# Turning h and the residual in the wide phases: TensorE transposes against 32 x 32 squares on VectorE

## The chip, the cores and the metric

The kernel runs on one core of a Trainium2 chip. The metric is the device time of one execution in microseconds (us), as the median of several runs. Beside the timed runs there is one execution under the hardware profiler; its rows and its trace are what this text reads.

The engines are named as the profile names them: PE is TensorE's matmul (PEld its weight loads), DVE is VectorE, ACT is ScalarE, POOL is GpSimd, SP is SyncE, which issues most of the transfers.

## The reference: what is computed

A two-layer decoder trunk on 256 positions of width 2048, in float32. Layer 0 is a sparse attention mixer and a SwiGLU block, layer 1 a pooling mixer and a SwiGLU block; every block is preceded by an RMSNorm and added to the residual. The part that the change touches, cut to what matters (D_FF is 5632):

```python
def rms_norm(x, g):
    x32 = x.astype(jnp.float32)
    y = x32 * lax.rsqrt(jnp.mean(x32 * x32, axis=-1, keepdims=True) + EPS)
    return (y * g.astype(jnp.float32)).astype(x.dtype)
...
def swiglu(h, w_gu, w_down):
    gu = h @ w_gu
    gate, up = gu[..., :D_FF], gu[..., D_FF:]
    return (jax.nn.silu(gate) * up) @ w_down
...
        h = rms_norm(x, norm_ffn[i])
        x = x + swiglu(h, ffn_w_gu[i], ffn_w_down[i])
    return rms_norm(x, norm_final)
```

## The kernel before

All weights stream through once. SyncE loads blocks of 128 x 1024 float32 (512 KB) into five buffers `wraw`. Each block is split into two float32r numbers: ScalarE copies the high part into `whi` (L158), VectorE subtracts it and leaves the rest in `wlo` (L159). There are three pairs of `whi` and `wlo`. A product of float32 accuracy is then three matmuls: high by high, high by low, low by high.

The first 376 us or so are the attention. Behind it come the wide phases, which the change is about: output projection, SwiGLU of layer 0, pooling mixer, SwiGLU of layer 1. They are products of all 256 positions (two halves `t` of 128) with 512 columns of a weight at a time, `wide_gemm` (L207). The activations are stationary (128 x 128), a block of weights holds two steps k of 128 rows by 512 columns, and each step and half takes the three matmuls of L216, L217 and L218. A block is thus 12 matmuls. The results of the two halves stand in two banks of PSUM with the positions on the partitions.

Work moves ahead of use in `next_block` (L173): when block b is about to be used, `ahead(b)` emits the split of block b + 2 and the load of block b + 4. The split of block b + 2 can start once block b - 1 has been used, since it takes that block's pair of buffers.

A result with positions on the partitions has to be turned before it can be stationary in the next product, which contracts over its columns. This is done in two places:

- `ffn` (L752): for each of 11 groups f of 512 columns there is a gate product `pg`, a Silu on ScalarE (L760), an up product `pu`, and `h` on VectorE (L764). Then eight 128 x 128 transposes on TensorE (L771) turn the two halves of `h` into PSUM tiles `turn`, and `split_pair` (L747) makes the split `hid` of them, in two steps of 128 x 512 on ScalarE (L749) and on VectorE (L750). `hid` is what the down product contracts over, 44 steps k.
- `residual` (L719): the product is added to the residual `xs` (L724), its squares are summed (L727), and eight transposes (L737) turn the new columns into `turn`. `spread` (L250) multiplies by the gain and splits into `xg[c]`, four steps k of the next phase's operand (L253 on ScalarE, L254 on VectorE).

There are 11 groups f in each of two layers, so 22 turns of `h`, 176 transposes. The residual is turned after four products of the output projection, four of layer 0's down product and four of the pooling's output, so 12 turns, 96 transposes. The last layer's down product turns nothing. Its last 512 columns use weights that were parked ahead in `xg` (L150), and `finish` (L789) applies the last norm. `row_scale` (L706) works out 1/rms of each row during the first product of each phase that follows a norm; its result is used only behind that product.

A scheduler sets the order of instructions on each engine from the program's order and dependences. It puts the transposes of a group between the matmuls of the next product.

The last layer's final gain is loaded into the buffers of `h` while its down product runs (L778).

Of the kernel before, what the change touches and what calls it, by code (L numbers as in the profile page):

```python
# [11 lines left out]
F32 = mybir.dt.float32  # L12
F32R = mybir.dt.float32r
AF = mybir.ActivationFunctionType
OP = mybir.AluOpType
AX = mybir.AxisListType

P = 128
D = 2048
S = 256  # L20
# [11 lines left out]
FT = DFF // P  # L32
# [13 lines left out]
N5 = 512  # L46
NJ = D // N5
FJ = DFF // N5
# [19 lines left out]
def nsa_pool_trunk(ctx, tc, first, xn, small, band, gfin, w_qk, w_vg, w1k, w1v, w_o,  # L68
                   p_in, p_grp, p_out, gu, down, out):
    nc = tc.nc  # L70
# [64 lines left out]
    state = {"dma": 0, "split": 0, "used": 0, "acc": 0, "more": None, "turn": 4}  # L135
# [11 lines left out]
    def emit_split(b):  # L147
        _, n, off = stream[b]
        t = raws.pop(b)
        if b in parked:  # L150
            for c in range(2):
                hi, lo = xg[4 * parked[b] + 2 * c:4 * parked[b] + 2 * c + 2]
                w = t[:, c * N5:(c + 1) * N5]
                nc.scalar.activation(hi, w, AF.Copy)
                nc.vector.tensor_tensor(lo, w, hi.bitcast(F32), op=OP.subtract)
            return
        hi, lo = split_tiles(off)
        nc.scalar.activation(hi[:, :n], t[:, :n], AF.Copy)  # L158
        nc.vector.tensor_tensor(lo[:, :n], t[:, :n], hi[:, :n].bitcast(F32), op=OP.subtract)  # L159
        parts[b] = (hi, lo)  # L160

    def ahead(b):
# [7 lines left out]
            emit_dma(state["dma"])  # L170
            state["dma"] += 1

    def next_block():  # L173
        while True:
            b = state["used"]
            ahead(b)
            state["used"] += 1
            if b not in parked:
                return parts.pop(b)


# [22 lines left out]
                k += 1  # L204
        return ps

    def wide_gemm(rhs, own=False, apart=0):  # L207

        ps = [bank(own) for _ in range(2)]
        n = len(rhs)

        def step(k, hi, lo, t):
            xa, xb = (rhs[k][:, a * S + t * P:a * S + (t + 1) * P] for a in range(2))
            nc.tensor.matmul(ps[t], xa, hi, start=k == 0, stop=False)  # L216
            nc.tensor.matmul(ps[t], xa, lo, start=False, stop=False)  # L217
            nc.tensor.matmul(ps[t], xb, hi, start=False, stop=k == n - 1)  # L218

        for k in range(n - apart):  # L220
            if k % 2 == 0:
                w = next_block()
            for t in range(2):
                step(k, *(a[:, k % 2 * N5:(k % 2 + 1) * N5] for a in w), t)
        for t in range(2):
            for i in range(apart):
                step(n - apart + i, *xg[2 * i:2 * i + 2], t)
        return ps
# [9 lines left out]
    ident = cst.tile([P, P], F32, name="ident")  # L238
# [7 lines left out]
    xg = [xgp.tile([P, 2 * S], F32R, name=f"xg{c}") for c in range(KC)]  # L246
# [3 lines left out]
    def spread(c, x, gain):  # L250

        f = col(gain, c) if isinstance(gain, str) else gain
        nc.scalar.activation(xg[c][:, :S], x, AF.Copy, scale=f)  # L253
        nc.vector.scalar_tensor_tensor(xg[c][:, S:], x, f, xg[c][:, :S].bitcast(F32),  # L254
                                       op0=OP.mult, op1=OP.subtract)
# [447 lines left out]
    def turn():  # L703
        return psT.tile([P, 2 * S], F32, name="turn")

    def row_scale():  # L706
# [9 lines left out]
        nc.vector.tensor_tensor(t, t, a, op=OP.mult)  # L716
        nc.vector.scalar_tensor_tensor(rcol, t, 1.5, rcol, op0=OP.add, op1=OP.mult)

    def residual(j, ps, gain, gf=None):  # L719


        xc = [xs[:, t, j * N5:(j + 1) * N5] for t in range(2)]
        for t in range(2):
            nc.vector.tensor_tensor(xc[t], ps[t], xc[t], op=OP.add)  # L724
        for t in range(2):
            sq = xp.tile([P, N5], F32, name="sq", bufs=2)
            nc.scalar.activation(sq, xc[t], AF.Square, accum_out=ssq[:, t, j:j + 1])  # L727
        if gf is not None:
            for t in range(2):
                nc.gpsimd.tensor_tensor(xc[t], xc[t], gf[j], op=OP.mult)  # L730
            return
        for q in range(2):
            tr = turn()
            for i in range(2):
                for t in range(2):
                    o = (2 * q + i) * P
                    nc.tensor.transpose(tr[:, i * S + t * P:i * S + (t + 1) * P], xc[t][:, o:o + P],  # L737
                                        ident)
            for i in range(2):
                spread(4 * j + 2 * q + i, tr[:, i * S:(i + 1) * S], gain)  # L740

    def pairs(pool, n, name):

        both = [pool.tile([P, 2, 2 * S], F32R, name=f"{name}{i}") for i in range(n // 2)]
        return both, [both[c // 2][:, c % 2] for c in range(n)]

    def split_pair(dst, tr):  # L747
        src = tr.rearrange("p (c t) -> p c t", c=2)
        nc.scalar.activation(dst[:, :, :S], src, AF.Copy)  # L749
        nc.vector.tensor_tensor(dst[:, :, S:], src, dst[:, :, :S].bitcast(F32), op=OP.subtract)  # L750

    def ffn(gain, fpool):  # L752
        hid2, hid = pairs(fpool, FT, "hid")
        for f in range(FJ):
            pg = wide_gemm(xg)
            if f == 0:
                row_scale()
            sg = [fpool.tile([P, N5], F32, name=f"sg{t}", bufs=1) for t in range(2)]
            for t in range(2):
                nc.scalar.activation(sg[t], pg[t], AF.Silu, scale=rcol[:, t:t + 1])  # L760
            pu = wide_gemm(xg)
            h = [fpool.tile([P, N5], F32, name="h", bufs=4) for t in range(2)]
            for t in range(2):
                nc.vector.scalar_tensor_tensor(h[t], pu[t], rcol[:, t:t + 1], sg[t], op0=OP.mult,  # L764
                                               op1=OP.mult)
            for q in range(2):
                tr = turn()
                for i in range(2):
                    for t in range(2):
                        o = (2 * q + i) * P  # L770
                        nc.tensor.transpose(tr[:, i * S + t * P:i * S + (t + 1) * P],  # L771
                                            h[t][:, o:o + P], ident)
                split_pair(hid2[2 * f + q], tr)
        gf = None
        if gain is None:
            gf = [fpool.tile([P, N5], F32, name="h", bufs=4) for _ in range(NJ)]
            for j in range(NJ):
                nc.sync.dma_start(gf[j], gfin[:, j * N5:(j + 1) * N5])  # L778

            nc.scalar.activation(fpool.tile([P, 1], F32, name="root"), sg[1][:, 0:1], AF.Sqrt,  # L780
                                 scale=0.0, bias=eps)
        for j in range(NJ - (gf is not None)):
            residual(j, wide_gemm(hid), gain, gf)
        if gf is not None:
            ps = wide_gemm(hid, apart=2 * PARK)
            for t in range(2):
                finish(t, ps[t], gf[NJ - 1], fpool)
# [26 lines left out]
                out[t * P:(t + 1) * P, i * N5:(i + 1) * N5], y)  # L814

    for j in range(NJ):
        residual(j, wide_gemm(oT, own=j == 0), "g_ffn0")
    op.close()

    with tc.tile_pool(name="f0", bufs=1, reuse_waits="tile") as fpool:  # L820
# [3 lines left out]
    with tc.tile_pool(name="pl", bufs=1, reuse_waits="tile") as pl:  # L824
# [8 lines left out]
        mixed = [pl.tile([P, 2 * S], F32R, name=f"mixed{c}") for c in range(KC)]  # L833

        def pool_group(g, first):
            ps = wide_gemm(xg)
            if first:
                row_scale()
            uh = [pl.tile([P, N5], F32R, name=f"uh{t}", bufs=2) for t in range(2)]
            ul = [pl.tile([P, N5], F32R, name=f"ul{t}", bufs=2) for t in range(2)]  # L840
            for t in range(2):
                r = rcol[:, t:t + 1]
                nc.scalar.activation(uh[t], ps[t], AF.Copy, scale=r)
                nc.vector.scalar_tensor_tensor(ul[t], ps[t], r, uh[t].bitcast(F32), op0=OP.mult,
                                               op1=OP.subtract)
            for q in range(2):
                tr = turn()
                for i in range(2):
                    a = slice((2 * q + i) * P, (2 * q + i + 1) * P)
                    d = tr[:, i * S:(i + 1) * S]  # L850
                    nc.tensor.matmul(d, uh[0][:, a], bh[:, g, :S], start=True, stop=False)
                    nc.tensor.matmul(d, ul[0][:, a], bh[:, g, :S], start=False, stop=False)
                    nc.tensor.matmul(d[:, :CS], uh[0][:, a], bl[:, g], start=False, stop=False)
                    nc.tensor.matmul(d[:, P:], uh[1][:, a], bh[:, g, S:], start=False, stop=False)
                    nc.tensor.matmul(d[:, P:], ul[1][:, a], bh[:, g, S:], start=False, stop=True)
                split_pair(pooled2[2 * g + q], tr)
# [19 lines left out]
        mix_group(GROUPS[-1])  # L876
        rhs = [mixed[4 * g + c] for g in GROUPS for c in range(4)]
        for j in range(NJ):
            residual(j, wide_gemm(rhs), "g_ffn1")

    with tc.tile_pool(name="f1", bufs=1, reuse_waits="tile") as fpool:
        ffn(None, fpool)
# [124 lines left out]
```

## Time and profile before

| | |
|---|---|
| median of 3 runs | 2127.1 us (2126.83 to 2128.48) |
| the profiled execution | 2126.66 us |
| its span, first to last instruction | 2124.9 us |
| granted TensorE clock | 0.999 |
| TensorE matmul busy | 2110.7 us, 99% |
| VectorE busy | 1182.8 us, 56% |
| ScalarE busy | 1030.0 us, 48% |
| transfers | 396.93 MB, 187 GB/s |

Matmuls are pipelined: a row's length is its latency and overlaps the next one's, so the time that an instruction takes from the stream is read from start to start. Each row of a group of instructions gives: line, engine, operation, output and inputs, shapes, count, then busy us, mean ns of one, and the idle time of the engine ahead of them with what ended it. A row of a timeline gives start and length in us.

### The profile page before, as it was taken

Reading aid. Unit: us, or ns where it says so; the run is one execution under the profiler, and the core shown is the slowest. Engines: PE = TensorE matmul, PEld = TensorE weight load, DVE = VectorE, ACT = ScalarE, POOL = GpSimd, SP = SyncE. Lnnn points to the kernel's source line nnn. Section 1 sums busy time; section 2 is a strip of 40 time slices with the busy share of each in tenths; the row PEclk is TensorE's granted clock in tenths of the full one; section 3 lists DMA queues with packets and bytes.
Section 4 is the critical chain, followed back from the end, with each engine's and each line's share of the span. In section 5 each row is a group of like instructions: output and inputs, shape, how many; then the busy total and the mean of one; then the engine's idle time right before and its main releaser. Section 6 shows DMA issues by size and latency. Waiting matters only on the chain.

```text
span 2124.9 us, 28354 instructions
## 1 busy us (share of the span) xinstructions
PE 2110.7 (99%) x10922; PEld 1810.6 (85%) x10922; DVE 1182.8 (56%) x1555; ACT 1030.0 (48%) x1492; POOL 53.6 (3%) x103
## 2 busy tenths in 40 slices
PE   9999999999999999999999999999999999999998
PEld 8999999888888888888888888888888888888886
DVE  8678887554554445545445555555444554455443
ACT  6567777454444444444444455444444444444442
POOL 1001111000000000000000000000000000000000
PEclk9999999999999999999999999999999999999999
DMA  6664444666666666666666656666666666677663
GB/s 246 209 219 137 144 143 128 210 187 191 192 185 192 188 189 189 187 191 191 193 189 191 198 175 183 184 192 183 193 188 190 190 187 191 188 220 224 195 192 106
DMA packets 114537, 396.93 MB, mean 187 GB/s; under 512 B 13378, under 2 KB 17730, under 8 KB 114146
## 3 DMA queue, kind: packets, MB, share of 16 engines
q1 hardware_dynamic: 113922, 394.41, 61.6%
q8 instruction: 85, 1.39, 0.3%
q10 hardware_dynamic: 480, 0.72, 0.1%
q14 instruction: 50, 0.41, 0.1%
HBM read 391.25 MB, written 2.16 MB: 185 GB/s over the span
## 4 chain that ended last, share of the span: by engine, by line
PE 98%; ACT 1%; DVE 1%; DMA 0%; issue 0%; SPq 0%; DVEq 0%
PE acc L216 27%; PE acc L218 27%; PE acc L217 27%; PE acc L194 3%; PE acc L192 3%; PE acc L193 3%; PE turn L771 1%; PE ps_o L665 1%; PE ps_t L627 1%; PE ps_s L559 1%; PE ps_s L560 1%; PE ps_s L561 1%; PE turn L737 0%; PE acc L499 0%; PE acc L500 0%; PE acc L501 0%
## 5 line engine op out<-in xcount | busy, mean ns | idle before, releaser
L159 DVE TENSOR_TENSOR wlo<-wraw,whi 128x1024 fp32r<-128x1024 f32 (+1 forms) x714 | 874.1, 1225 | 828.5 <-ACT whi L158 823.9
L158 ACT ACTIVATE whi<-wraw 128x1024 fp32r<-128x1024 f32 (+1 forms) x714 | 754.3, 1057 | 914.8 <-PE acc L218 826.8
L218 PE MATMUL acc<-whi,xg 128*128 128x512 f32 x1536 | 599.9, 391 | 0.0
L217 PE MATMUL acc<-wlo,xg 128*128 128x512 f32 x1536 | 598.8, 390 | 0.0
L216 PE MATMUL acc<-whi,xg 128*128 128x512 f32 x1536 | 546.3, 391 | 0.0
L217 PEld LDWEIGHTS acc<-wlo,xg 128*128 128x128 f32 x1536 | 288.5, 188 | 59.1
L218 PEld LDWEIGHTS acc<-whi,xg 128*128 128x128 f32 x1536 | 288.6, 188 | 58.7
L216 PEld LDWEIGHTS acc<-whi,xg 128*128 128x128 f32 x1536 | 288.6, 188 | 58.1
L217 PE MATMUL acc<-wlo,hid 128*128 128x512 f32 x688 | 268.3, 390 | 0.0
L218 PE MATMUL acc<-whi,hid 128*128 128x512 f32 x688 | 268.0, 390 | 0.0
L216 PE MATMUL acc<-whi,hid 128*128 128x512 f32 x688 | 242.0, 390 | 0.0
L192 PE MATMUL acc<-xg,whi 128*128 128x256 f32 x560 | 158.2, 286 | 0.5 <-ACT whi L327 0.3
L193 PE MATMUL acc<-xg,whi 128*128 128x256 f32 x560 | 157.2, 284 | 0.0
L194 PE MATMUL acc<-xg,wlo 128*128 128x256 f32 x560 | 154.3, 285 | 1.4 <-DVE wlo L159 1.2
L217 PEld LDWEIGHTS acc<-wlo,hid 128*128 128x128 f32 x688 | 129.2, 188 | 26.7
L218 PEld LDWEIGHTS acc<-whi,hid 128*128 128x128 f32 x688 | 129.2, 188 | 26.6
L216 PEld LDWEIGHTS acc<-whi,hid 128*128 128x128 f32 x688 | 129.2, 188 | 26.4
L192 PEld LDWEIGHTS acc<-xg,whi 128*128 128x128 f32 x560 | 105.8, 189 | 1.9 <-ACT whi L327 1.4
L193 PEld LDWEIGHTS acc<-xg,whi 128*128 128x128 f32 x560 | 105.9, 190 | 0.0
L194 PEld LDWEIGHTS acc<-xg,wlo 128*128 128x128 f32 x560 | 103.6, 189 | 2.6 <-DVE wlo L159 1.4
L587 ACT ACTIVATE prob<-prob,mx 128x128 f32<-128x128 f32 (+1 forms) x128 | 56.5, 444 | 9.9 <-DVE mx L581 6.8
L217 PE MATMUL acc<-wlo,oT 128*128 128x512 f32 x128 | 50.2, 392 | 0.0
(235 smaller groups left out, 1784.0 us busy)
## 6 DMA issues: line engine op xcount, KB each, us to landing
wraw<-in_gu SPq DMA_DIRECT2D x352, 512.0 KB, 3.7
wraw<-in_down SPq DMA_DIRECT2D x176, 512.0 KB, 3.8
wraw<-in_w_qk SPq DMA_DIRECT2D x64, 512.0 KB, 4.2
wraw<-in_w_o SPq DMA_DIRECT2D x32, 512.0 KB, 3.6
wraw<-in_p_in SPq DMA_DIRECT2D x32, 512.0 KB, 3.6
wraw<-in_p_out SPq DMA_DIRECT2D x32, 512.0 KB, 3.6
bias<-skew SPq DMA_DIRECT2D x32, 200.0 KB, 3.2
wx<-in_first SPq DMA_DIRECT2D x15, 320.0 KB, 6.6
```

The source lines that it names most:

```text
L158: nc.scalar.activation(hi[:, :n], t[:, :n], AF.Copy)
L159: nc.vector.tensor_tensor(lo[:, :n], t[:, :n], hi[:, :n].bitcast(F32), op=OP.subtract)
L192: nc.tensor.matmul(ps, hi, x[:, :S], start=first, stop=False)
L193: nc.tensor.matmul(ps, hi, x[:, S:], start=False, stop=False)
L194: nc.tensor.matmul(ps, lo, x[:, :S], start=False, stop=last)
L216: nc.tensor.matmul(ps[t], xa, hi, start=k == 0, stop=False)
L217: nc.tensor.matmul(ps[t], xa, lo, start=False, stop=False)
L218: nc.tensor.matmul(ps[t], xb, hi, start=False, stop=k == n - 1)
L559: nc.tensor.matmul(o, q[0], k[0], start=True, stop=False)
L560: nc.tensor.matmul(o, q[0], k[1], start=False, stop=False)
L561: nc.tensor.matmul(o, q[1], k[0], start=False, stop=True)
L587: nc.scalar.activation(p[:, o:o + n], p[:, o:o + n], AF.Exp, bias=mx[:, i:i + 1], accum_out=su[:, i:i + 1])
```

## The change

The turns leave TensorE. A new function `turned_squares` cuts the turn of 512 columns by 256 positions into squares of 32 x 32. One VectorE instruction (`nc.vector.transpose`, L742 in the new kernel, STREAM_TRANSPOSE in the order) reads 32 partitions of the source, eight squares wide (2 x 4 x 32 elements), transposes each square and writes it to another quarter of the partitions of one tile `flip`. 16 such instructions, for each of four source quarters and four destination quarters, make a turn. They are not emitted at once but put on a list `later`. `next_block(beside)` takes that many entries off the list behind each block's split, not ahead of the latest `wlo` instruction (`tc.issue_after`), and `wide_gemm` empties the rest of the list at its end.

- `h`: two entries a block (`beside=2`) during the next product, four during the first gate product of a phase. The split of the turned `h` is one entry at the list's end, now one step of 128 x 1024 on each of ScalarE and VectorE (`split_four`).
- the residual: 16 squares and four spreads, 20 entries, at four a block in the output projection, in the pooling phase and in the first gate products, at two a block in layer 0's down product.
- `ffn(None)`, the last layer: the list is emptied by a call of `some()` ahead of the last down product, since the buffers of `h` are then loaded with the final gain; that load is now two transfers of 512 KB instead of four of 256 KB.

```diff
+    later = []
+
+    def some(n=None):
+        with tc.issue_after(state["lo"]):
+            for f in later[:n]:
+                f()
+        del later[:n]
+
-    def next_block():
+    def next_block(beside=0):
         while True:
             b = state["used"]
             ahead(b)
             state["used"] += 1
             if b not in parked:
+                some(beside)
                 return parts.pop(b)
...
             if k % 2 == 0:
-                w = next_block()
+                w = next_block(beside)
             for t in range(2):
                 step(k, *(a[:, k % 2 * N5:(k % 2 + 1) * N5] for a in w), t)
+        some()
...
+    flip = xp.tile([P, 4, S], F32, name="flip")
+
+    def turned_squares(src, dst=flip):
+        to = dst.rearrange("p c (t i s) -> i p t c s", t=2, i=4)
+        of = src.rearrange("p t (c j s) -> j p t c s", c=4, j=4)
+        for i in range(4):
+            for j in range(4):
+                a, b = (slice(32 * q, 32 * q + 32) for q in (i, j))
+                later.append(lambda o=to[i][b], x=of[j][a]: nc.vector.transpose(o, x))
...
-        for q in range(2):
-            tr = turn()
-            for i in range(2):
-                for t in range(2):
-                    o = (2 * q + i) * P
-                    nc.tensor.transpose(tr[:, i * S + t * P:i * S + (t + 1) * P], xc[t][:, o:o + P],
-                                        ident)
-            for i in range(2):
-                spread(4 * j + 2 * q + i, tr[:, i * S:(i + 1) * S], gain)
+        turned_squares(xs[:, :, j * N5:(j + 1) * N5])
+        for c in range(4 * j, 4 * j + 4):
+            later.append(lambda c=c: spread(c, flip[:, c % 4], gain))
...
         for f in range(FJ):
-            pg = wide_gemm(xg)
+            pg = wide_gemm(xg, beside=2 if f else 4)
...
-            for q in range(2):
-                tr = turn()
-                for i in range(2):
-                    for t in range(2):
-                        o = (2 * q + i) * P
-                        nc.tensor.transpose(tr[:, i * S + t * P:i * S + (t + 1) * P],
-                                            h[t][:, o:o + P], ident)
-                split_pair(hid2[2 * f + q], tr)
+            turned_squares(h)
+            later.append(lambda f=f: split_four(hid4[f]))
         gf = None
         if gain is None:
-            gf = [fpool.tile([P, N5], F32, name="h", bufs=4) for _ in range(NJ)]
-            for j in range(NJ):
-                nc.sync.dma_start(gf[j], gfin[:, j * N5:(j + 1) * N5])
+            some()
+            gf = []
+            for j in range(0, NJ, 2):
+                g2 = fpool.tile([P, 2, N5], F32, name="h", bufs=2)
+                nc.sync.dma_start(g2, gfin[:, j * N5:(j + 2) * N5])
+                gf += [g2[:, 0], g2[:, 1]]
...
-            residual(j, wide_gemm(hid), gain, gf)
+            residual(j, wide_gemm(hid, beside=2), gain, gf)
...
-        residual(j, wide_gemm(oT, own=j == 0), "g_ffn0")
+        residual(j, wide_gemm(oT, own=j == 0, beside=4), "g_ffn0")
...
-            ps = wide_gemm(xg)
+            ps = wide_gemm(xg, beside=4)
...
-            residual(j, wide_gemm(rhs), "g_ffn1")
+            residual(j, wide_gemm(rhs, beside=4), "g_ffn1")
```

How this moves the instructions is seen in their order (line, operation, output and inputs, shape, and a count where equal ones stand in a row). TensorE, behind the first `h` of layer 0, before; `turn` is the PSUM tile, `ident` the identity:

```order
L216 MATMUL acc<-whi,xg_83 128x512
L217 MATMUL acc<-wlo,xg_83 128x512
L218 MATMUL acc<-whi,xg_83 128x512
L771 MATMUL turn<-ident,h 128x128 x2
L216 MATMUL acc<-whi,xg_83 128x512
L217 MATMUL acc<-wlo,xg_83 128x512
L771 MATMUL turn<-ident,h 128x128 x6
L218 MATMUL acc<-whi,xg_83 128x512
```

In the new kernel no row with `ident` and `h` or `xs` is left on TensorE; the matmuls stand as they stood, some with the halves t in another order. VectorE at the start of layer 0's SwiGLU, where the last turned columns of the residual become `xg_92` to `xg_95` (steps k = 12 to 15 of the product that has just begun). Before:

```order
L724 TENSOR_TENSOR xs<-acc,xs 128x512 x2
L159 TENSOR_TENSOR wlo<-wraw,whi 128x1024
L711 TENSOR_REDUCE tot<-ssq 128x2
L713 TENSOR_SCALAR na<-tot 128x2
L714 RECIPROCAL rcol<-nt 128x2
L715 SCALAR_TENSOR_TENSOR nt<-rcol 128x2
L716 TENSOR_TENSOR nt<-nt,na 128x2
L717 SCALAR_TENSOR_TENSOR rcol<-nt,rcol 128x2
L159 TENSOR_TENSOR wlo<-wraw,whi 128x1024
L254 SCALAR_TENSOR_TENSOR xg_92<-turn,sm,xg_92 128x256
L254 SCALAR_TENSOR_TENSOR xg_94<-turn,sm,xg_94 128x256
```

And in the new kernel at the same place, from the second of its five splits on:

```order
L159 TENSOR_TENSOR wlo<-wraw,whi 128x1024
L742 STREAM_TRANSPOSE flip<-xs 32x2x4x32 x4
L726 TENSOR_SCALAR na<-tot 128x2
L727 RECIPROCAL rcol<-nt 128x2
L159 TENSOR_TENSOR wlo<-wraw,whi 128x1024
L742 STREAM_TRANSPOSE flip<-xs 32x2x4x32 x4
L728 SCALAR_TENSOR_TENSOR nt<-rcol 128x2
L159 TENSOR_TENSOR wlo<-wraw,whi 128x1024
L742 STREAM_TRANSPOSE flip<-xs 32x2x4x32 x4
L729 TENSOR_TENSOR nt<-nt,na 128x2
L159 TENSOR_TENSOR wlo<-wraw,whi 128x1024
L730 SCALAR_TENSOR_TENSOR rcol<-nt,rcol 128x2
L267 SCALAR_TENSOR_TENSOR xg_92<-flip,sm,xg_92 128x256
```

`xg_92` stood behind two splits of the new product and now stands behind five, with 16 squares among them. VectorE behind the last `h` of the last layer, before:

```order
L764 SCALAR_TENSOR_TENSOR h<-acc,rcol,sg_16177 128x512
L764 SCALAR_TENSOR_TENSOR h<-acc,rcol,sg_16178 128x512
L159 TENSOR_TENSOR wlo<-wraw,whi 128x1024 x2
L750 TENSOR_TENSOR hid_12879<-turn,hid_12879 128x2x256
L750 TENSOR_TENSOR hid_12880<-turn,hid_12880 128x2x256
L159 TENSOR_TENSOR wlo<-wraw,whi 128x1024
```

And in the new kernel:

```order
L789 SCALAR_TENSOR_TENSOR h<-acc,rcol,sg_16291 128x512
L789 SCALAR_TENSOR_TENSOR h<-acc,rcol,sg_16292 128x512
L159 TENSOR_TENSOR wlo<-wraw,whi 128x1024
L742 STREAM_TRANSPOSE flip<-h 32x2x4x32 x16
L159 TENSOR_TENSOR wlo<-wraw,whi 128x1024 x2
L777 TENSOR_TENSOR hid_12940<-flip,hid_12940 128x4x256
```

Here the 16 squares stand together, between the split of the down product's block 2 (blocks counted from 0) and that of block 3.

More of the change, by code (lines that the diff above doesn't have):

```diff
@@ L158, in emit_split @@
         nc.scalar.activation(hi[:, :n], t[:, :n], AF.Copy)
-        nc.vector.tensor_tensor(lo[:, :n], t[:, :n], hi[:, :n].bitcast(F32), op=OP.subtract)
+        state["lo"] = nc.vector.tensor_tensor(lo[:, :n], t[:, :n], hi[:, :n].bitcast(F32),
+                                              op=OP.subtract).ins
         parts[b] = (hi, lo)
@@ L205, in gemm, with wide_gemm @@
         return ps
-    def wide_gemm(rhs, own=False, apart=0):
+    def wide_gemm(rhs, own=False, apart=0, beside=0):
         ps = [bank(own) for _ in range(2)]
@@ L752, in ffn, with split_four @@
     def ffn(gain, fpool):
-        hid2, hid = pairs(fpool, FT, "hid")
+        hid4 = [fpool.tile([P, 4, 2 * S], F32R, name=f"hid{f}") for f in range(FJ)]
+        hid = [hid4[c // 4][:, c % 4] for c in range(FT)]
+        def split_four(t):
+            nc.scalar.activation(t[:, :, :S], flip, AF.Copy)
+            nc.vector.tensor_tensor(t[:, :, S:], flip, t[:, :, :S].bitcast(F32), op=OP.subtract)
         for f in range(FJ):
-            pg = wide_gemm(xg)
+            pg = wide_gemm(xg, beside=2 if f else 4)
             if f == 0:
@@ L760, in ffn @@
                 nc.scalar.activation(sg[t], pg[t], AF.Silu, scale=rcol[:, t:t + 1])
-            pu = wide_gemm(xg)
-            h = [fpool.tile([P, N5], F32, name="h", bufs=4) for t in range(2)]
+            pu = wide_gemm(xg, beside=2)
+            h = fpool.tile([P, 2, N5], F32, name="h", bufs=2)
             for t in range(2):
-                nc.vector.scalar_tensor_tensor(h[t], pu[t], rcol[:, t:t + 1], sg[t], op0=OP.mult,
+                nc.vector.scalar_tensor_tensor(h[:, t], pu[t], rcol[:, t:t + 1], sg[t], op0=OP.mult,
                                                op1=OP.mult)
-            for q in range(2):
-                tr = turn()
-                for i in range(2):
-                    for t in range(2):
-                        o = (2 * q + i) * P
-                        nc.tensor.transpose(tr[:, i * S + t * P:i * S + (t + 1) * P],
-                                            h[t][:, o:o + P], ident)
-                split_pair(hid2[2 * f + q], tr)
+            turned_squares(h)
+            later.append(lambda f=f: split_four(hid4[f]))
         gf = None
         if gain is None:
-            gf = [fpool.tile([P, N5], F32, name="h", bufs=4) for _ in range(NJ)]
-            for j in range(NJ):
-                nc.sync.dma_start(gf[j], gfin[:, j * N5:(j + 1) * N5])
+            some()
[4 more added lines that the diff above has]
+                gf += [g2[:, 0], g2[:, 1]]
             nc.scalar.activation(fpool.tile([P, 1], F32, name="root"), sg[1][:, 0:1], AF.Sqrt,
```

## The prediction

> **What bounds the kernel now.** I read the page first, then who waited for whom on TensorE, then the timelines of VectorE and TensorE. The page's busy row and its chain row:
>
> ```profile
> PE 2110.7 (99%) x10922; PEld 1810.6 (85%) x10922; DVE 1182.8 (56%) x1555; ACT 1030.0 (48%) x1492; POOL 53.6 (3%) x103
> PE 98%; ACT 1%; DVE 1%; DMA 0%; issue 0%; SPq 0%; DVEq 0%
> ```
>
> A busy TensorE proves little by itself, so the waits matter. The view has seven rows for TensorE; the first and the last:
>
> ```profile
> PE acc L310 <- DVE warm L307: 1.3, 1, 1.3
> ...
> PE acc L194 <- DVE wlo L328: 0.2, 1, 0.2
> ```
>
> The largest is 1.3 us, and none of the seven is a wait of the wide products (L216 to L218) for a split. VectorE and ScalarE are idle half the time. So the wide phases last as long as TensorE's instruction stream, and whatever leaves that stream is saved, provided the side work still arrives in time. The changed lines' groups of transposes on TensorE:
>
> ```profile
> L771 PE MATMUL turn<-ident,h 128*128 128x128 f32 x176 | 26.3, 272 | 0.0
> L737 PE MATMUL turn<-ident,xs 128*128 128x128 f32 x96 | 14.4, 272 | 0.0
> ```
>
> The 272 ns are latency; they overlap. What a transpose costs is seen in start times. TensorE around the first eight, matmuls between them left out:
>
> ```profile
> 494.75 0.39 PE L218 MATMUL acc<-whi,xg 128*128 128x512 f32 x1
> ...
> 494.99 0.38 PE L771 MATMUL turn<-ident,h 128*128 128x128 f32 x2
> ...
> 495.67 0.82 PE L771 MATMUL turn<-ident,h 128*128 128x128 f32 x6
> ...
> 496.56 0.40 PE L216 MATMUL acc<-whi,xg 128*128 128x512 f32 x1
> ```
>
> From 494.75 to 496.56 there are 1.81 us for four matmul steps and eight transposes. The step itself comes from a stretch that has no transposes: the last layer's down product, 264 matmuls between two additions of the residual (columns: start, length).
>
> ```profile
> 1936.28 1.28 DVE L724 TENSOR_TENSOR xs<-acc,xs 128x512 f32<-128x512 f32 x2
> ...
> 1996.12 1.28 DVE L724 TENSOR_TENSOR xs<-acc,xs 128x512 f32<-128x512 f32 x2
> ```
>
> 59.84 us / 264 = 0.2267 us a matmul. Four are 0.91, so the eight transposes took 0.90.
>
> **What is removed.** The same down product in the first layer has eight transposes, and a gate-and-up pair has 192 matmuls and eight transposes:
>
> ```profile
> 994.95 1.28 DVE L724 TENSOR_TENSOR xs<-acc,xs 128x512 f32<-128x512 f32 x2
> ...
> 1055.71 1.28 DVE L724 TENSOR_TENSOR xs<-acc,xs 128x512 f32<-128x512 f32 x2
> ```
> ```profile
> 489.94 1.40 DVE L764 SCALAR_TENSOR_TENSOR h<-acc,rcol,sg 128x512 f32<-128x512 f32 x2
> ...
> 534.36 0.74 DVE L764 SCALAR_TENSOR_TENSOR h<-acc,rcol,sg 128x512 f32<-128x512 f32 x1
> ```
>
> 60.76 - 59.84 = 0.92; 44.42 - 192 x 0.2267 = 0.90 (periods in a row average 44.43, so 0.91). There are 176/8 = 22 groups for h and 96/8 = 12 for the residual: 22 x 0.91 + 12 x 0.92 = **31.0 us removed**, if TensorE never waits for what replaces them.
>
> **What is added.** 34 x 16 = 544 squares on VectorE, each 32 partitions x 256 elements. The trace has no such operation. The nearest rows are 128 and 256 elements from one source, 256 elements on 32 partitions, and, as the far end, a slow operation:
>
> ```profile
> L595 DVE TENSOR_SCALAR prob<-prob,su 128x128 f32<-128x128 f32 x64 | 15.6, 285 | 0.1
> L646 DVE CAST tcm<-ps_t 96x256 fp32r<-96x256 f32 x16 | 6.7, 418 | 7.5 <-PE ps_t L643 7.4
> L335 DVE TENSOR_TENSOR kf<-acc,rst 32x256 f32<-32x256 f32 x6 | 2.6, 426 | 0.1
> L531 DVE RECIPROCAL gall<-gall 128x192 f32<-128x192 f32 x1 | 1.4, 1352 | 0.0
> ```
>
> So 0.42 us is the near end; 1352/192 x 256 = 1.80 us the far one. I take 0.42: a square moves data as the cast does, and from 285 to 418 ns for 128 more elements is one element a VectorE cycle. What counts in a row of squares is start to start, and the trace shows two ways, full-width pairs and a step between partition groups:
>
> ```profile
> 62.86 0.42 DVE L334 TENSOR_TENSOR kf<-acc,rst 96x256 f32<-96x256 f32 x1 [0.61 <-PE acc L194]
> 63.30 0.43 DVE L335 TENSOR_TENSOR kf<-acc,rst 32x256 f32<-32x256 f32 x1
> ```
> ```profile
> L750 DVE TENSOR_TENSOR hid<-turn,hid 128x512 fp32r<-128x512 f32 x44 | 28.3, 686 | 30.3 <-ACT hid L749 30.3
> ```
> ```profile
> 496.82 1.29 DVE L750 TENSOR_TENSOR hid<-turn,hid 128x512 fp32r<-128x512 f32 x2 [1.37 <-ACT hid L749]
> ```
>
> The pair on all partitions takes 1.29 us where two lengths make 1.37: the second starts 0.08 early. The pair that changes quarters starts 0.44 apart at a length of 0.42: no overlap. Consecutive squares change their output quarter, so I take s = 0.44 us from start to start; 0.34 is the lower end. The Trainium skill (VectorE: DVE Perf Modes, "Two Vector instructions with no wait between them") says that an instruction is held until all earlier ones end when its start quadrant differs from the last one's; both pairs agree. By this rule s is 0.44, without it 0.34. The same page ("The three transpose paths") gives 311 ns for a 128x128 bf16 VectorE transpose; with 128 more elements at 0.96 GHz that makes an estimate of 0.44, of which no run here shows anything yet.
>
> Whether this is hidden depends on where it stands. Times from the start of a product, at the last down product (first the rows of VectorE, then of TensorE):
>
> ```profile
> 1874.39 1.23 DVE L159 TENSOR_TENSOR wlo<-wraw,whi 128x1024 fp32r<-128x1024 f32 x1 [1.49 <-ACT whi L158]
> 1875.53 1.40 DVE L764 SCALAR_TENSOR_TENSOR h<-acc,rcol,sg 128x512 f32<-128x512 f32 x2
> 1877.11 1.22 DVE L159 TENSOR_TENSOR wlo<-wraw,whi 128x1024 fp32r<-128x1024 f32 x1 [0.17 <-ACT whi L158]
> 1879.83 1.23 DVE L159 TENSOR_TENSOR wlo<-wraw,whi 128x1024 fp32r<-128x1024 f32 x1 [1.50 <-ACT whi L158]
> ```
> ```profile
> 1875.82 0.62 PE L216 MATMUL acc<-whi,hid 128*128 128x512 f32 x2
> ...
> 1884.43 0.39 PE L217 MATMUL acc<-wlo,hid 128*128 128x512 f32 x1
> ```
>
> A block is 12 matmuls, 2.72 us. Block 2's lo is made 1.29 us after the product starts and is first read two matmuls into block 2, at 5.44 + 0.45. A lo costs 1.15 start to start (1874.39 to 1875.53). I number blocks within the product.
>
> *Two squares per split* (pairs of gate and up, first down product): 1.15 + 2 x 0.44 = 2.03 < 2.72. Hidden.
>
> *Four per split, no new phase* (three products of the output projection, three of the pooling's): 1.15 + 1.76 = 2.91 a block, four blocks in a row. Block 6's lo ends at 1.29 + 5 x 1.15 + 16s = 14.1 and is read at 6 x 2.72 + 0.45 = 16.8. Slack 2.7; hidden until s = 0.61.
>
> *Four per split at a phase start* (three: the first gate product of each layer and the first pooling product read, at k = 12, the columns just turned). The row-scale steps are put among the squares; first and last of six:
>
> ```profile
> 448.30 0.16 DVE L711 TENSOR_REDUCE tot<-ssq 128x2 f32<-128x8 f32 x1
> ...
> 450.50 0.16 DVE L717 SCALAR_TENSOR_TENSOR rcol<-nt,rcol 128x2 f32<-128x2 f32 x1
> ```
> ```profile
> L254 DVE SCALAR_TENSOR_TENSOR xg<-turn,sm,xg 128x256 fp32r<-128x256 f32 x48 | 21.0, 478 | 8.8 <-ACT xg L253 8.7
> ```
>
> Six at 0.2 add 1.2, the first spread 0.48: 1.29 + 5.75 + 7.04 + 1.2 + 0.48 = 15.8. That half is read four matmuls into block 6, at 17.2. Slack 1.4; hidden until s = 0.53.
>
> *The burst.* Before the last down product the list is emptied at once: 16 squares between block 2's lo and block 3's. Block 3's lo ends at 1877.11 + 1.15 + 16s + 1.23 = 1879.49 + 16s; the matmul that reads it was at 1884.43. TensorE waits 16s - 4.94: **2.1 us**. It is the only term on the path, between 0.5 (s = 0.34) and tens of microseconds.
>
> The rest is nothing: one split of 128x1024 replaces two of 128x512 on ScalarE and VectorE; spreads read SBUF instead of PSUM; SP's second load of the final gain waits for the last square, but the weight block behind it needs the buffer that block 3's lo frees later still. The weights' loads have room:
>
> ```profile
> wraw<-in_gu SPq DMA_DIRECT2D x352, 512.0 KB, 3.7
> ```
>
> the load of block b + 5 waits for block b's lo, which ended 2.5 us into block b - 2; 3.7 more is 6.2, and the split that needs it starts with block b + 3, 13.6 us in. 7.4 us of lateness are free.
>
> The sum: -31.0 + 2.1 = -28.9. The profiled execution took 2126.66 us (span 2124.9 plus 1.8 outside): 2097.8, span 2096.0. The median of the runs is 0.4 above it: **2098.2 us**.
>
> **The rivals.**
> 1. *No stall worth naming*: squares overlap (s = 0.34). The saving stands nearly whole: 2127.1 - 31.0 + 0.5 = 2096.6. For it, the L750 pair; against it, the step between partition groups. 7%.
> 2. *Two cycles an element*: a block may have to be filled and then drained, where L595 and L646 show one cycle for plain moves; s is then 0.44 + 0.27 = 0.71. Lost: burst 6.4, three phase starts 16 x (0.71 - 0.53) = 2.9 each, six others 1.6 each: 24.7. Time 2120.8. 7%.
> 3. *VectorE becomes the limit: slower.* The same sum is 160s - 88.9 us (3 x 16, 6 x 16 and 16 squares). It exceeds 31.0 from s = 0.75 on. At three cycles an element, s = 0.97, it is 66.3: 2162.4. For it: the reciprocal shows that some VectorE operations take six cycles. Against: a square computes nothing. 7%.
> 4. *The idle slows TensorE's clock.* At the kernel's start 256-column matmuls stand 0.21 us apart, later 0.12, also behind a wait:
>
> ```profile
> 5.73 0.42 PE L192 MATMUL acc<-xg,whi 128*128 128x256 f32 x1
> 5.94 0.41 PE L193 MATMUL acc<-xg,whi 128*128 128x256 f32 x1
> ...
> 43.31 0.39 PE L194 MATMUL acc<-xg,wlo 128*128 128x256 f32 x1 [1.18 <-DVE wlo L159]
> 43.53 0.28 PE L192 MATMUL acc<-xg,whi 128*128 128x256 f32 x1
> 43.65 0.28 PE L193 MATMUL acc<-xg,whi 128*128 128x256 f32 x1
> ```
>
> If the 2.1 us pause brings that state back, and for 5 us (an estimate: the start's slow steps still stand at 5.7), half of that is lost: +2.5, 2100.7. Against it: 0.2 us behind a wait of 1.18 us the steps are 0.12 again. 5%. The Trainium skill (TensorE: Matmul & The Clock Gate, "Part 1") puts the idle that halves the clock at about 3.4 us; by that rule this needs s above 0.52.
>
> That the change does not take the transposes off TensorE is excluded by the order of instructions.
>
> **How the numbers follow.** The forecast has 74%. The range reaches below rival 1 by 1.6 us for the unknown of the sum, to 2095.0, and up to s = 0.60 (burst 4.7, phase starts 1.1 each: 8.0 lost, 2104.1) and rival 4 on top of it, 2106.6, rounded up to 2107.0. Outside lie rivals 2 and 3 and a rest. 0.2% is 4.3 us, about what a measurement of this kernel can tell from no change. Rival 2 falls partly into it (s = 0.72 to 0.78). Faster 0.89, same 0.04, slower 0.07.
>
> **What would show it.** Right: 544 transposes of about 0.42 us on VectorE, 0.44 apart; periods of 43.5 and 59.8 us instead of 44.4 and 60.8; one wait of TensorE for a lo of about 2 us, near 1855 us (1884.4 less the saving so far), and none at the phase starts. Wrong: squares longer than 0.5 us, waits for lo or xg at block 6 of the nine products with four squares per split, or a step between matmuls other than 0.2267 us.

## The result and the profile after

| | before | after |
|---|---|---|
| median of the runs | 2127.6 us (2126.8 to 2128.5, 4 runs) | 2101.9 us (2099.8 to 2102.9, 4 runs) |
| profiled execution, its span | 2124.9 | 2100.0 (2101.8 with what lies around it) |

The ratio is 0.9878 (95% interval 0.9861 to 0.9895): 25.7 us faster than before, and 3.7 us above the forecast 2098.2. The times of before are the three of the first table and one more run.

The page of the new kernel, busy row and chain row:

```profile
PE 2082.6 (99%) x10650; PEld 1783.5 (85%) x10650; DVE 1407.9 (67%) x2077; ACT 1030.5 (49%) x1470; POOL 51.9 (2%) x103
PE 96%; DVE 1%; ACT 1%; DMA 1%; issue 0%; SPq 0%; DVEq 0%
```

TensorE lost its 272 transposes (10922 to 10650 matmuls), VectorE's busy share rose from 56% to 67%, and TensorE is still the chain. The groups that took the transposes' place, count, sum and mean ns of one (in the new kernel the wide products' lines are L228 to L230, the turned squares L742, the additions into `h` L789 and into the residual L749):

```profile
L742 DVE STREAM_TRANSPOSE flip<-h 32x256 f32<-32x256 f32 x352 | 153.3, 436 | 7.1
L742 DVE STREAM_TRANSPOSE flip<-xs 32x256 f32<-32x256 f32 x192 | 83.6, 436 | 3.3
```

352 + 192 = 544 squares of 436 ns. The steady periods, from VectorE's timeline: one gate-and-up pair, and one down product of the first layer:

```profile
488.22 1.40 DVE L789 SCALAR_TENSOR_TENSOR h<-acc,rcol,sg 128x512 f32<-128x512 f32 x2
...
531.74 0.74 DVE L789 SCALAR_TENSOR_TENSOR h<-acc,rcol,sg 128x512 f32<-128x512 f32 x1
...
983.26 1.28 DVE L749 TENSOR_TENSOR xs<-acc,xs 128x512 f32<-128x512 f32 x2
...
1043.10 1.28 DVE L749 TENSOR_TENSOR xs<-acc,xs 128x512 f32<-128x512 f32 x2
```

43.52 us instead of 44.42, and 59.84 instead of 60.76: the 31.0 us did leave the path, and nothing in those phases took their place. But the span fell by 24.9 only, so 6.1 us came back somewhere. The waits of TensorE name the first suspect (total, count, longest):

```profile
PE acc L229 <- DVE wlo L159: 3.0, 2, 2.1
PE acc L323 <- DVE warm L320: 1.3, 1, 1.3
```

Before, no wide product waited for a split; now two do, for 2.15 and 0.87 us. **The first is the burst.** VectorE, from the last `h` on:

```profile
1847.42 1.40 DVE L789 SCALAR_TENSOR_TENSOR h<-acc,rcol,sg 128x512 f32<-128x512 f32 x2
1849.00 1.23 DVE L159 TENSOR_TENSOR wlo<-wraw,whi 128x1024 fp32r<-128x1024 f32 x1 [0.18 <-ACT whi L158]
1850.14 7.17 DVE L742 STREAM_TRANSPOSE flip<-h 32x256 f32<-32x256 f32 x16
1857.35 2.36 DVE L159 TENSOR_TENSOR wlo<-wraw,whi 128x1024 fp32r<-128x1024 f32 x2
```

Sixteen squares in 7.17 us, fifteen steps and one length: (7.17 - 0.44) / 15 = 0.449 us from start to start. TensorE in the same place:

```profile
1855.87 0.61 PE L228 MATMUL acc<-whi,hid 128*128 128x512 f32 x2
1858.63 0.50 PE L229 MATMUL acc<-wlo,hid 128*128 128x512 f32 x1 [2.15 <-DVE wlo L159]
...
1860.06 0.63 PE L229 MATMUL acc<-wlo,hid 128*128 128x512 f32 x1
1860.48 0.63 PE L230 MATMUL acc<-whi,hid 128*128 128x512 f32 x1
...
1863.53 0.39 PE L229 MATMUL acc<-wlo,hid 128*128 128x512 f32 x1
1863.76 0.40 PE L230 MATMUL acc<-whi,hid 128*128 128x512 f32 x1
```

The wait is the forecast one. What was forecast only as a rival stands behind it: at 1860 the step between matmuls is 0.42 to 0.43 us, almost twice the usual 0.23, and at 1863.5 it is 0.23 again. Busy time by stretches (the stretch and its length, the busy time of PE, PEld, DVE, ACT and POOL with the number of instructions, then the granted clock of TensorE, the share of the DMA engines and GB/s):

```profile
1859.00:1860.00 1.00, 1.00 (x5) 0.83 (x4) 1.00 (x2) 0.36 (x1) 0.00 (x0) 0.84 0.96 324
1860.00:1861.00 1.00, 1.00 (x4) 0.74 (x3) 1.00 (x2) 0.00 (x0) 0.00 (x0) 0.50 1.00 283
...
1862.00:1863.00 1.00, 1.00 (x3) 0.75 (x3) 0.00 (x0) 0.57 (x1) 0.00 (x0) 0.50 0.83 258
1863.00:1864.00 1.00, 1.00 (x5) 0.78 (x4) 0.48 (x1) 0.64 (x2) 0.00 (x0) 0.95 1.03 344
```

The clock was half for 0.32 + 3 + 0.1 = 3.4 us, from 1859.7 to 1863.1. In this time TensorE runs eight steps that are 0.2 us too long, so it loses 1.6 us. What the burst costs in all is read from the distance between the last residual addition ahead of a SwiGLU and the first one of its down product: 542.63 us in the last layer (1368.70 to 1911.33) against 538.56 for the same work in the first (444.70 to 983.26), 4.07 us. Of these, 2.31 are the step with the wait, 0.11 the step behind it (0.34 instead of 0.23, as behind every wait here), and 1.6 the clock.

**The second wait** stands where none was forecast, in the second product of the output projection. VectorE:

```profile
379.97 0.68 DVE L749 TENSOR_TENSOR xs<-acc,xs 128x512 f32<-128x512 f32 x1
383.31 0.69 DVE L749 TENSOR_TENSOR xs<-acc,xs 128x512 f32<-128x512 f32 x1 [2.65 <-DMA xs<-in_xn]
384.03 1.78 DVE L742 STREAM_TRANSPOSE flip<-xs 32x256 f32<-32x256 f32 x4
385.85 1.23 DVE L159 TENSOR_TENSOR wlo<-wraw,whi 128x1024 fp32r<-128x1024 f32 x1
387.10 1.78 DVE L742 STREAM_TRANSPOSE flip<-xs 32x256 f32<-32x256 f32 x4
388.92 1.22 DVE L159 TENSOR_TENSOR wlo<-wraw,whi 128x1024 fp32r<-128x1024 f32 x1
```

And TensorE:

```profile
385.65 0.61 PE L228 MATMUL acc<-whi,oT 128*128 128x512 f32 x2
387.13 0.50 PE L229 MATMUL acc<-wlo,oT 128*128 128x512 f32 x1 [0.87 <-DVE wlo L159]
...
390.19 0.50 PE L229 MATMUL acc<-wlo,oT 128*128 128x512 f32 x1
...
393.27 0.50 PE L229 MATMUL acc<-wlo,oT 128*128 128x512 f32 x1
```

The second half of the first residual addition waits until 383.31 for its load. Four squares stand between it and the split that TensorE reads next, so that split ends at 387.1. From there on a block costs VectorE 388.92 - 385.85 = 3.07 us and TensorE 2.72, so TensorE waits a little once a block until the list is empty. The starts of the matmuls that read the split are 3.06 and 3.08 us apart. The four steps are 1.25, 0.44, 0.45 and 0.41 us instead of 0.23 each, 1.64 too long, with 0.11 behind each: 2.1 us. Then 4.07 + 2.1 = 6.2, which is the 6.1 that came back.

### The profile page after: what moved, and what is told of

The parts are those of the page before. It is cut to its first block, busy times and chain, and to the rows that moved or that the text cites. A ratio compares the mean times of both kernels' runs of the same rounds, so it can differ in the third digit from the quotient of the medians.

```text
span 2100.0 us, 28308 instructions
## 1 busy us (share of the span) xinstructions
PE 2082.6 (99%) x10650; PEld 1783.5 (85%) x10650; DVE 1407.9 (67%) x2077; ACT 1030.5 (49%) x1470; POOL 51.9 (2%) x103
## 4 chain that ended last, share of the span: by engine, by line
PE 96%; DVE 1%; ACT 1%; DMA 1%; issue 0%; SPq 0%; DVEq 0%
PE acc L229 27%; PE acc L230 27%; PE acc L228 27%; PE acc L205 3%; PE acc L203 3%; PE acc L204 3%; PE ps_t L640 1%; PE ps_o L678 1%; PE ps_s L572 1%; PE ps_s L573 1%; PE ps_s L574 1%; DVE flip L742 1%; DMA xs<-in_xn 0%; PE acc L512 0%; PE acc L513 0%
## 5 line engine op out<-in xcount | busy, mean ns | idle before, releaser
L159 DVE TENSOR_TENSOR wlo<-wraw,whi 128x1024 fp32r<-128x1024 f32 (+1 forms) x714 | 873.2, 1224 | 609.4 <-ACT whi L158 607.0
L230 PE MATMUL acc<-whi,xg 128*128 128x512 f32 x1536 | 596.6, 389 | 0.0
L228 PE MATMUL acc<-whi,xg 128*128 128x512 f32 x1536 | 536.2, 389 | 0.0
L228 PEld LDWEIGHTS acc<-whi,xg 128*128 128x128 f32 x1536 | 288.3, 188 | 59.9
L230 PEld LDWEIGHTS acc<-whi,xg 128*128 128x128 f32 x1536 | 288.3, 188 | 59.8
L230 PE MATMUL acc<-whi,hid 128*128 128x512 f32 x688 | 268.1, 390 | 0.0
L228 PE MATMUL acc<-whi,hid 128*128 128x512 f32 x688 | 240.6, 390 | 0.0
L742 DVE STREAM_TRANSPOSE flip<-h 32x256 f32<-32x256 f32 x352 | 153.3, 436 | 7.1
L228 PEld LDWEIGHTS acc<-whi,hid 128*128 128x128 f32 x688 | 129.6, 188 | 27.0
L230 PEld LDWEIGHTS acc<-whi,hid 128*128 128x128 f32 x688 | 129.4, 188 | 27.1
L742 DVE STREAM_TRANSPOSE flip<-xs 32x256 f32<-32x256 f32 x192 | 83.6, 436 | 3.3
```

Source lines behind the costliest of these rows:

```text
L159: state["lo"] = nc.vector.tensor_tensor(lo[:, :n], t[:, :n], hi[:, :n].bitcast(F32), op=OP.subtract).ins
L742: later.append(lambda o=to[i][b], x=of[j][a]: nc.vector.transpose(o, x))
```

## The experiments

The theory after the result: all of the 31.0 us is saved; the burst gives back 4.1 us (pause and half clock), four squares per split behind the late load 2.1 us, and nothing else is on the path. The rivals: the burst costs its pause alone and the rest has another cause; or squares cost TensorE something wherever they are. Each kernel is compared with runs of the kernel before on the same chip, 2126.8 us in the first series (2126.7 to 2128.3, 7 runs) and 2127.0 in the second (2126.4 to 2128.1, 8 runs).

### The burst spread over the down product

```diff
-        gf = None
+        gf = early = None
         if gain is None:
-            some()
+            early = wide_gemm(hid, beside=2)
...
-            residual(j, wide_gemm(hid, beside=2), gain, gf)
+            ps = early if j == 0 and early else wide_gemm(hid, beside=2)
+            residual(j, ps, gain, gf)
```

> Edit: the last layer's 16 squares are not emptied at once but taken two per split during the last down product; the final gain is loaded behind that product. Theory A (the saving is whole, 31.0 us, and is given back at two places: about 4.1 us at the burst, of which 2.15 is the wait for a split, 0.3 the restart and 1.6 a halved TensorE clock, and about 2.1 us in the output projection): TensorE's wait near 1858 us is gone, no stretch of granted clock 0.50 there, and the time falls by 4.1 us, from 2101.9 to about 2097.8. Rival B (the shortfall is spread over the whole kernel, the two places are only where it shows): the time falls by the 2.15 us of the wait at most, or by less than 1 us.

Measured: 2098.3 us (2097.4 to 2099.2), ratio 0.9862 (0.9846 to 0.9879). VectorE where the burst was:

```profile
1850.41 1.23 DVE L159 TENSOR_TENSOR wlo<-wraw,whi 128x1024 fp32r<-128x1024 f32 x1 [0.18 <-ACT whi L158]
1851.55 0.87 DVE L742 STREAM_TRANSPOSE flip<-h 32x256 f32<-32x256 f32 x2
1853.13 1.23 DVE L159 TENSOR_TENSOR wlo<-wraw,whi 128x1024 fp32r<-128x1024 f32 x1 [0.70 <-ACT whi L158]
```

With two squares between splits VectorE waits for ScalarE again, so it has time to spare, and TensorE has no wait there. The distance that was 542.63 is 538.56: all 4.07 us are back. The profiled span fell by only 2.6, to 2097.4, because the same half clock now stands in another place, in the attention:

```profile
96.00:97.00 1.00, 0.26 (x2) 0.17 (x2) 0.97 (x3) 1.00 (x4) 0.00 (x0) 1.00 0.98 246
...
99.00:100.00 1.00, 0.69 (x6) 0.69 (x7) 0.16 (x1) 0.80 (x4) 0.00 (x0) 0.84 0.76 278
100.00:101.00 1.00, 1.00 (x6) 1.00 (x5) 0.00 (x0) 0.13 (x1) 0.00 (x0) 0.50 0.72 164
```

Nothing before 370 us differs between the two kernels, so this is no effect of the edit; the last section comes back to it. The medians differ by 3.6; three of the four runs have a granted clock of 0.999, against 0.998 in the profiled one, so most of them seem to be without this stretch.

### Two squares per split in the output projection

```diff
-        residual(j, wide_gemm(oT, own=j == 0, beside=4), "g_ffn0")
+        residual(j, wide_gemm(oT, own=j == 0, beside=2), "g_ffn0")
```

> Edit: the output projection takes two entries per split instead of four. Theory A: VectorE then needs about 2.15 us a block against TensorE's 2.72, so the late start (the first residual waits for its load) is made up and not kept; the 2.1 us go down to at most 0.5, the time falls by 1.6 to 2.1 us to about 2100. Rival B: no change, or a new wait at the first gate product, since the last turned columns come later.

Measured: 2101.9 us (2101.7 to 2103.5), ratio 0.9882 (0.9867 to 0.9897): no change against the new kernel's 2101.9. The waits in the output projection are gone, but another has come, as rival B had it. VectorE and TensorE at the first gate product:

```profile
444.94 1.22 DVE L159 TENSOR_TENSOR wlo<-wraw,whi 128x1024 fp32r<-128x1024 f32 x1
446.07 1.67 DVE L267 SCALAR_TENSOR_TENSOR xg<-flip,sm,xg 128x256 fp32r<-128x256 f32 x4
...
460.30 1.22 DVE L159 TENSOR_TENSOR wlo<-wraw,whi 128x1024 fp32r<-128x1024 f32 x1
461.44 1.67 DVE L267 SCALAR_TENSOR_TENSOR xg<-flip,sm,xg 128x256 fp32r<-128x256 f32 x4
```
```profile
461.97 0.74 PE L230 MATMUL acc<-whi,xg 128*128 128x512 f32 x2 [0.86 <-DVE xg L267]
```

At two per split the list of the third product is not empty when the gate product begins: four spreads, 1.67 us, are left over and run ahead of the squares, and one split more (460.30) comes ahead of the new columns' spreads than in the new kernel, 1.1 us. The prediction had put the slack of that phase start at 1.4 us. It is used up, and the long steps that end at 457.2, 460.4 and 462.0 cost 1.9 us, with the steps beside them. The 2.1 us have not been saved, only moved.

### Both together

The two diffs above in one kernel.

> Both edits. Theory A: 31.0 us saved and next to nothing given back: 6 us below the changed kernel, about 2096, granted clock 0.999. Rival B: within 2 us of the changed kernel.

Measured: 2098.1 us (2097.7 to 2099.4), ratio 0.9864 (0.9849 to 0.9879), as the burst spread alone. The 1.9 us at the gate product are there again (long steps that end at 458.9, 462.1 and 463.7). What the first two experiments showed adds up; that the whole 2.1 us of the output projection would come free was wrong.

### Two and three per split

The second product, which has the late load, gets two squares per split, the others three, so that the list is empty when the gate product begins; the burst is spread as above.

```diff
-        residual(j, wide_gemm(oT, own=j == 0, beside=4), "g_ffn0")
+        residual(j, wide_gemm(oT, own=j == 0, beside=2 if j == 1 else 3), "g_ffn0")
```

> The last layer's squares two per split, as in the first experiment, and the output projection with two entries per split in its second product and three in its third and fourth, so that no turned columns are left over at the start of the first gate product. Theory A (everything not saved is lost at named waits): no wait of TensorE on a split or on xg behind 376 us; the span is that of before less 31.0, 2093.9 us, or 1.7 us more if a window of halved clock falls into the attention, as it did in the first and third experiments; time about 2096 to 2097.5. Rival B (a part of the shortfall has another cause): no faster than the experiment with both edits, 2098.1.

Measured: 2096.0 us (2095.1 to 2097.5), ratio 0.9852 (0.9836 to 0.9868), the lowest median of all kernels here. The end of TensorE's list of waits:

```profile
PE acc L203 <- ACT whi L340: 0.8, 2, 0.5
PE acc L513 <- DVE wlo L159: 0.7, 1, 0.7
PE acc L228 <- ACT oT L702: 0.5, 1, 0.5
PE acc L205 <- DVE wlo L341: 0.2, 1, 0.2
```

No wide product waits for a split or for turned columns, and behind 379 us no step between matmuls is longer than 0.36 us. The profiled span is 2095.7; it has one stretch of half clock in the attention, at 100.1, worth 1.7 us. 2124.9 - 31.0 + 1.7 = 2095.6. With this the 31.0 us are found whole, and the places where they were given back are known.

### The squares for h alone

The residual's transposes go back to TensorE; only `h` is turned on VectorE.

```diff
-        turned_squares(xs[:, :, j * N5:(j + 1) * N5])
-        for c in range(4 * j, 4 * j + 4):
-            later.append(lambda c=c: spread(c, flip[:, c % 4], gain))
+        for q in range(2):
+            tr = turn()
+            for i in range(2):
+                for t in range(2):
+                    o = (2 * q + i) * P
+                    nc.tensor.transpose(tr[:, i * S + t * P:i * S + (t + 1) * P], xc[t][:, o:o + P],
+                                        ident)
+            for i in range(2):
+                spread(4 * j + 2 * q + i, tr[:, i * S:(i + 1) * S], gain)
```

> Edit: one part of the change alone, h in squares on VectorE, the residual turned on TensorE as before. Theory A: 22 x 0.91 = 20.0 us saved, the burst's 4.1 us lost, no loss in the output projection: 2126.8 - 20.0 + 4.1 = 2110.9. If the residual's part of the change (11.0 us saved, 2.1 lost) were worth nothing, this would be as fast as the changed kernel, 2101.9.

Measured: 2110.6 us (2109.2 to 2111.3, 5 runs), ratio 0.9921 (0.9907 to 0.9935). The output projection has no wait, as the theory has it. 2124.9 - 22 x 0.91 + 2.4 for the burst + 1.7 for a half clock = 2109.0; the span is 2108.8. The burst's wait is the same, and yet no half clock follows it:

```profile
1867.00:1868.00 1.00, 0.00 (x0) 0.00 (x0) 0.96 (x3) 0.30 (x1) 0.00 (x0) 1.00 0.00 0
1868.00:1869.00 1.00, 0.02 (x1) 0.03 (x1) 1.00 (x2) 1.00 (x2) 0.00 (x0) 1.00 0.18 57
1869.00:1870.00 1.00, 1.00 (x4) 0.83 (x5) 1.00 (x2) 0.70 (x1) 0.00 (x0) 1.00 0.91 250
1870.00:1871.00 1.00, 1.00 (x6) 0.81 (x5) 1.00 (x2) 0.00 (x0) 0.00 (x0) 1.00 0.88 299
```

(TensorE: `[2.15 <-DVE wlo L159]` at 1868.98.) The 1.7 us of this profile stand in the attention, at 99.2. So a pause of 2.15 us brings the half clock in one kernel and not in the other; its length alone does not decide.

### All squares at once

```diff
-                some(beside)
+                some(20 if beside else 0)
```

> Edit: the list is emptied at each place behind the next split, as in the burst, instead of two or four entries a block. Theory A: each of the 33 other turns then costs TensorE about what the burst costs, 2.5 us without and 4.1 us with the halved clock: 80 to 135 us more than the changed kernel, 2182 to 2237, slower than before the change. Rival C (VectorE has time anyway, the spreading is worth nothing): within 5 us of the changed kernel.

Measured: 2221.6 us (2221.1 to 2223.0), ratio 1.0444 (1.0429 to 1.0460). One row of TensorE's waits tells it:

```profile
PE acc L229 <- DVE wlo L159: 77.3, 34, 6.1
```

The 34 groups of squares make 34 waits. 77.3 us of waiting, 34 x 0.27 for the restart (2.31 + 0.11 - 2.15, as at the burst), and 24 times 3.41 us at half clock (23 stretches, one of which is twice as long), 1.6 us each as at the burst: 77.3 + 9.2 + 38.4 = 124.9. Without any of it the span would be 2093.9; it is 2219.8, 125.9 more. The same instructions in another order are 94.8 us slower than before the change: the squares pay only where they are spread among the splits, and then they cost TensorE nothing.

### Shorter bursts

Fourteen squares, then twelve, at the place of the burst, the rest two per split; the diff is that of the burst spread, with one line more, `some(12)` or `some(10)` ahead of `early = ...` (the first split then adds two).

> Edit: 14 squares in the burst. TensorE waits 14 x 0.449 - 4.94 = 1.35 us. This places the pause at which the clock falls: with 3.4 us at 0.50 behind it, a pause of 1.35 us is enough; without, it lies between 1.35 and 2.15 us.

> Edit: 12 instead of 16 squares in the burst, the others two per split behind it. By 16s - 4.94 with the measured 0.449 us a square, TensorE waits 0.4 us. Theory A with a clock that falls on a pause of somewhere between 1.2 and 2.15 us: no stretch of half clock near 1858 us; the profiled span 3.4 us below the changed kernel's 2100.0. Rival (any wait there brings half clock): a stretch of 3.4 us at 0.50 remains.

Measured, one run each: 2099.5 us (span 2097.7) and 2099.0 (span 2097.2). The wait, in the kernel with fourteen:

```profile
1857.92 0.50 PE L229 MATMUL acc<-wlo,hid 128*128 128x512 f32 x1 [1.24 <-DVE wlo L159]
```

With twelve it is 0.35. So 0.35, 1.24 and 2.15 us for 12, 14 and 16 squares: 0.45 a square, on a line with the prediction's 16s - 4.94 with s = 0.449, less 0.1. Neither of the two profiles has a half clock between the start and the end of the program. The kernel with fourteen had been expected to place the pause at which the clock falls. It does not: a border of the windows that the last section describes stands at 1857.1 there and cuts the 1.24 us in two. The spans differ by 0.5 us where the waits differ by 0.9. Most of the rest is in the trace of the kernel with twelve, where four squares still stand between the splits: TensorE has a second long step there, which ends at 1865.53 and costs 0.32 us with the step behind it.

## Why the prediction was right, and where it was not

**What is removed.** Right: 31.0 us by the periods, and 2095.7 against 2095.6 in the kernel without the other losses.

**The price of a square.** Right: 0.436 us long and 0.449 apart, against 0.42 and 0.44. Rivals 1, 2 and 3 needed 0.34, 0.71 and 0.97. By the Trainium skill's rule on held instructions (VectorE: DVE Perf Modes, "Two Vector instructions with no wait between them") s was 0.44; the trace agrees, in a second pair too: in the output projection a full-width split starts 1.25 us before the square behind it (385.85 to 387.10), where two full-width operations stand 1.14 apart.

**The burst.** The wait was right, 2.15 us against 2.1. The term was too small all the same: 0.27 us for stopping and starting TensorE, and 1.6 for the clock. The prediction treated the slower clock as a case of its own with 5%, and in the profiled run it came on top of the forecast. Its argument against was that a wait of 1.18 us had left the clock alone; that row was too short to speak for 2.1 us. Its size, +2.5 for 5 us at half speed, was too large: 3.4 us and 1.6.

**Four per split, no new phase.** This step failed, in one of its six products. It took the splits to be on time when a product begins, 1.29 us in for block 2's, and asked only whether the squares let them fall behind. In the second product of the output projection VectorE itself waits for a load, and block 2's lo ends at 387.1, 1.0 us behind the time at which TensorE would have read it (two steps behind 385.65, at 386.1); the sum had it ready 5.89 - 1.29 = 4.6 us ahead of that. The profile of before had shown the wait, in VectorE's timeline:

```profile
380.18 0.69 DVE L724 TENSOR_TENSOR xs<-acc,xs 128x512 f32<-128x512 f32 x1
381.95 0.69 DVE L724 TENSOR_TENSOR xs<-acc,xs 128x512 f32<-128x512 f32 x1 [1.08 <-DMA xs<-in_xn]
384.74 1.22 DVE L159 TENSOR_TENSOR wlo<-wraw,whi 128x1024 fp32r<-128x1024 f32 x1 [2.10 <-ACT whi L158]
```

There it was harmless: VectorE was done 2.1 us before its next split could begin. The change put four squares, 1.8 us, behind that load, the load itself came 1.4 us later, and what had been slack was a wait. The load was issued no later (at 373.9, against 374.1 before), but it took 9.3 us to land instead of 7.8. In all eight kernels that turn the residual in squares it took 9.1 to 9.4, in the two others 7.8, so this comes with the change; why is not shown. The rate was then too slow to catch up: 3.07 us a block (2.91 in the prediction, which let the split overlap the square behind it) against TensorE's 2.72. In the other five products there was no wait, as forecast: their residual additions are 21.74 to 21.76 us apart. But at 3.07 us a block their slack was 2.1 us and not 2.7 (in the third product block 6's lo ends at 416.16 and is read at 418.24).

**The phase starts.** Right: no wait at the three of them. The slack was 1.7 us instead of 1.4 (in layer 0 the first spread ends at 460.49, and the matmul that reads it starts at 462.21). In the experiment with two squares per split, four left-over spreads and one more split, 2.8 us together, were too much for it.

**The sum.** 31.0 was right, what is given back was 6.1 us and not 2.1; so the time is 3.7 us above the forecast. It lies inside the range, whose upper part was there for a longer square and for the clock; that it had room for a late load too was luck.

## What to carry to other kernels

Work that is taken off the bounding engine and spread thinly among another engine's due work can cost nothing, while the same instructions in one lump cost more than they saved: count how many fit between two due times, not how busy the engine is. Before trusting "hidden", read from the trace when the helping engine really starts each stage; a wait of that engine that is harmless today is the place where added work first comes late. And when a lump is cured, look at what is left on the list at the next phase start.

## What the runs showed of the hardware

**TensorE's clock goes by windows of 3.413 us.** In the profile after, the clock's record stands at full speed from 6.24 us and falls at 1859.68: 543.0 x 3.4133 us later. Between the start of the program and its last 7 us, every stretch of half clock in the ten profiles is one such window long (one in the kernel with all squares at once is two), and every one begins a whole number of windows behind that profile's first change to full speed. Laying this grid over TensorE's timeline and summing its idle time in each window, with start and end of the program left out:

| idle in the window | windows | next window at half clock |
|---|---|---|
| 0.90 to 1.63 us | 26 | 0 |
| 1.64 to 1.86 us | 10 | 4 |
| 1.88 us and more | 25 | 25 |

So a little over half a window of idle is enough, in one pause or in several. One window does not fit: in the kernel with all squares at once, a window without any work was followed by one at half clock, and this one, with 0.82 us of idle, by a second at half clock. The table tells the two bursts apart: in the profile after, the 2.15 us lie whole between 1856.3 and 1859.7; with the squares for `h` alone a border at 1867.3 cuts them into 0.50 and 1.65. It tells the attention's cases apart too: its pauses give 1.64 to 1.71 us in one window where the clock fell, 0.92 and 0.92 in two windows in the profile after, where it did not. The grid's place differs from run to run, by which the same kernel has such windows or not; at 1.7 us each that would make the 1 to 3 us between runs of one kernel, but only profiled runs have a grid to look at. The granted clock of the other runs fits: in the new kernel it is 0.999 in the run of 2099.8 us, 0.998 in those of 2101.8 and 2102.0 and 0.997 in that of 2102.9, where one window at half clock makes 0.0008. That such windows are the cause is argued, not shown. What decides between 1.64 and 1.86 us stays open.

The Trainium skill (TensorE: Matmul & The Clock Gate, "Part 1") gives the window as 3413 ns and free-running; these runs agree. It puts the fall behind at least one idle window, about 3.4 us. Here the measurement decides: a pause of 2.15 us is enough if one window holds it.

**A restart costs 0.27 us beside the wait**: at the burst the step is 2.54 us for a wait of 2.15 and a usual step of 0.23, 0.16 more, and the next one is 0.34, 0.11 more.
